# Differential attention in 32 fixed steps of TensorE, with norms of seven heads together and RoPE on POOL

## The chip, the cores and the metric

The kernel runs on one core of one Trainium2 chip. A core has a matrix engine (TensorE, PE in the profile, with its weight loads as PEld), a vector engine (VectorE, DVE), an activation engine (ScalarE, ACT), a general engine (GpSimd, POOL) and SyncE (SP), which here issues all transfers. Each engine takes its own queue of instructions in order and meets the others through semaphores. TensorE reads SBUF and accumulates into the banks of PSUM; VectorE and ScalarE read both. The metric is the time on the device in microseconds, the median of several runs; lower is better.

## The reference, cut to what matters

Two layers of an encoder trunk over 512 tokens of width 1024. Each layer projects the residual stream once and feeds three branches: an SSD scan, a differential attention and a cross-attention into 256 memory tokens. Gates merge the three, an output projection and a LayerNorm close the layer. The change touches the second branch alone:

```python
q = _apply_rope(dq.reshape(Bsz, S, DIFF_HEADS, 2, DIFF_HEAD_DIM), cos, sin)
k = _apply_rope(dk.reshape(Bsz, S, DIFF_HEADS, 2, DIFF_HEAD_DIM), cos, sin)
v = dv.reshape(Bsz, S, DIFF_HEADS, 2 * DIFF_HEAD_DIM)
o = _diff_attention(q, k, v, lam)     # per head: (softmax(q0 k0) - lam * softmax(q1 k1)) v
o = _rmsnorm(o, diff_norm_w[layer]) * (1.0 - lambda_init)
y_diff = o.reshape(Bsz, S, DIFF_WIDTH) * jax.nn.silu(dg.astype(jnp.float32))
```

There are 8 heads. Each has two 64-wide maps (the 128 rows of a head's Q and K hold both) and a 128-wide value.

## The kernel before

**Numbers in two parts.** Every product keeps float32 accuracy by splitting both operands into a high and a low part (`split`, line 95: ScalarE rounds the high part, VectorE subtracts it) and adding three matmuls (`mm3`, line 107: low x high, high x low, high x high).

**Units of weight.** All large matrices come in units of 128 x 1024 numbers, 512 KB each. A plan lists functions with the unit that each needs (`T`, line 130). `emit` (line 133) walks it, and issues the loads (`wr`, two buffers) and splits (`wh`, `wl`, three buffers) of units two places ahead of their use. A projection (`proj`, line 161) takes one unit: 8 x 3 matmuls of 512 columns into one bank `pj`. V projections (`proj_tok`, line 174) take 48 matmuls of 256 columns per unit.

**Order of the work.** The framework orders the instructions of each engine by priorities, which follow the program's order, and by its own estimate of when operands and buffers are ready. `late(n)` (line 100) lowers a priority by `n` places. Inside `manual_schedule(engines={PE})` TensorE's instructions keep the order of the program among themselves; before the change that is used for the six score matmuls of a chunk (lines 866 to 871) and in the SSD branch. Transfers wait in SyncE's one queue in the order in which they were put there.

**The differential attention** (`diff`, line 779). The letters of `ORDER` (line 47, `"qk01vw"` and `"qkg01G"`) list the jobs of an even and of an odd place h:

- `rope` (line 804) projects Q or K of a head. ScalarE copies it out of PSUM (`rx`, line 810), four transfers swap the halves of each 64 rows (`rsw<-rx`, line 813), three VectorE instructions form x cos + swap(x) sin (lines 815 to 817), and `split` makes the two parts `q` or `k`.
- `vpart`, `gpart`: V of two heads, and the SiLU gate of a head (`sdy`).
- `att(h, qp)` (line 848) does two chunks of 128 queries. For each: six score matmuls, three products for each of two maps, into two of the four banks `pm`; a minimum over keys and an exponential with its sum for each map; the weighted difference (line 879); four transposes through the one bank `pt` (line 882); the split into `wT`. Then 12 matmuls with V (line 888) into a bank `po`, which a head holds from its first half to its second.
- At the end of each head (lines 892 to 912): square, four matmuls with a column of ones for the sum of squares, a chain of small VectorE instructions for the norm factor `r` (a 128 x 4 tile), and a transfer that writes it transposed to DRAM (`rd`). For the last head four matmuls spread `r` over a bank instead.
- `fin(h)` (line 915), among the gates of the branch's output (`branch_out`, line 642): broadcasts a head's `rd` to all partitions (`fth<-rd`), multiplies, and splits into `dy`, the input of the branch's projection.

Of the kernel before, what the change touches and what calls it, by code (L numbers as in the profile page):

```python
# [44 lines left out]
LX, LA, LD, LS = 70, 15, 80, 80  # L45

ORDER = ("qk01vw", "qkg01G")
# [10 lines left out]
class Net:  # L58
# [583 lines left out]
    def branch_out(self, l, pool, i, ub, y, tags, after=None, fin=None):  # L642

        st = {}
# [22 lines left out]
        for j in range(KC):  # L667
            if (i, j) in self.ahead_gates:
                self.T(r(j))
            else:  # L670
                self.T(g(j), (l, UGL + 8 * i + j))
            if fin is not None:
                self.T(fin(j))
# [105 lines left out]
    def diff(self, l):  # L779
# [3 lines left out]
        def begin():  # L783
# [17 lines left out]
            self.qk, self.v, self.rd = {}, {}, {}  # L801
            self.sdy = self.t(fp, [P, KC, S], "sdy", bufs=1)

        def rope(h, nm):
            def f(wh, wl):
                fp = self.fp
                ps = self.proj(wh, wl)
# [6 lines left out]
                o = self.t(fp, [P, S], "ro", bufs=1)  # L814
                self.tt(o, x, self.cos, ALU.mult)
                self.tt(sw, sw, self.sin, ALU.mult)
                self.tt(o, o, sw, ALU.add)

                self.qk[h, nm] = [self.t(fp, [P, S], f"{nm}{i}", F32R) for i in range(2)]
                self.split(*self.qk[h, nm], o)  # L820
            return f

        def vpart(h):
            def f(wh, wl):
                if h % 2 == 0:
                    self.vps = [self.bank(self.pj, "pj") for _ in range(2)]
                self.proj_tok(h % 2, wh, wl, *self.rows(self.xh, self.xl), self.vps)
# [8 lines left out]
            return f  # L836

        def gpart(h):
            def f(wh, wl):
                fp = self.fp  # L840
                ps = self.proj(wh, wl)
                th = self.t(fp, [P, S], "fth")
                self.act(th, ps, AF.Tanh, scale=0.5)
                g = self.sdy[:, h, :]
                self.stt(g, th, 1.0, ps, ALU.add, ALU.mult)
            return f

        def att(h, qp):
            def f():
                fp = self.fp  # L850
                (qh, ql), (kh, kl) = self.qk[h, "q"], self.qk[h, "k"]
                v, y = self.v[h], self.sdy[:, h, :]
                if qp == 0:
                    self.po = self.bank(self.pm, "pm")
                    self.s0 = self.t(fp, [P, 4], "fs0")
                po, s0 = self.po, self.s0
                wT = [self.t(fp, [P, 4, 2 * P], f"wT{i}", F32R) for i in range(2)]
                for i in range(2):
                    qc = 2 * qp + i
                    qs = slice(qc * P, (qc + 1) * P)  # L860
                    mx = self.t(fp, [P, 2], "fmx")
                    sm = self.t(fp, [P, 2], "fsm")
                    pp = self.t(fp, [P, 2, S], "fpp")

                    pss = [self.bank(self.pm, "pm") for _ in range(2)]
                    with self.tc.manual_schedule(engines={mybir.EngineType.PE}):
                        for n, (a, b) in enumerate(((ql, kh), (qh, kl), (qh, kh))):
                            for c in range(2):
                                rows = slice(64 * c, 64 * c + 64)
                                with self.late(-LS if n or c else 0):  # L870
                                    self.mm(pss[c], a[rows, qs], b[rows, :], n == 0, n == 2)
                    for c, ps in enumerate(pss):
                        nc.vector.tensor_reduce(out=mx[:, c:c + 1], in_=ps, axis=AX.X, op=ALU.min)  # L873
                        self.act(pp[:, c, :], ps, AF.Exp, scale=-1.0, bias=mx[:, c:c + 1],
                                 accum_out=s0[:, qc:qc + 1] if c == 0 else sm[:, 1:2])

                    nc.vector.reciprocal(out=sm[:, 1:2], in_=sm[:, 1:2])
                    self.ts(sm[:, 1:2], sm[:, 1:2], s0[:, qc:qc + 1], ALU.mult, self.nlam, ALU.mult)
                    self.stt(pp[:, 0, :], pp[:, 1, :], sm[:, 1:2], pp[:, 0, :], ALU.mult, ALU.add)
                    pt = self.bank(self.pt, "pt")  # L880
                    for kc in range(4):
                        self.tr(pt[:, kc * P:(kc + 1) * P], pp[:, 0, kc * P:(kc + 1) * P])
                    o = slice(i * P, (i + 1) * P)
                    self.split(wT[0][:, :, o], wT[1][:, :, o], pt.rearrange("p (k q) -> p k q", k=4))
                with self.late(LA):
                    for kc in range(4):
                        e = slice(kc * P, (kc + 1) * P)
                        self.mm3(po[:, 2 * qp * P:2 * (qp + 1) * P], v[0][:, e], v[1][:, e],
                                 wT[0][:, kc, :], wT[1][:, kc, :], kc == 0, kc == 3)
                if qp == 0:  # L890
                    return
                sq = self.t(fp, [P, S], "fth")
                self.act(sq, po, AF.Square)
                self.stt(y, po, self.dnw, y, ALU.mult, ALU.mult)
                pt = self.bank(self.pt, "pt")
                for c in range(4):
                    self.mm(pt[:, c:c + 1], sq[:, c * P:(c + 1) * P], self.ones[:, 0:1])
                nc.vector.reciprocal(out=s0, in_=s0)
                ms = self.t(fp, [P, 4], "fms")
                self.stt(ms, pt[:, 0:4], 1.0 / 128.0, s0, ALU.mult, ALU.mult)  # L900
                self.tt(ms, ms, s0, ALU.mult)
                self.ts(ms, ms, EPS, ALU.add)
                r = self.rsqrt(fp, ms, 4)
                self.tt(r, r, s0, ALU.mult)
                if h == KC - 1:

                    self.rd[h] = self.bank(self.pm, "pm")
                    for c in range(4):
                        self.mm(self.rd[h][:, c * P:(c + 1) * P], bc(r[:, c:c + 1], [P, P]), self.ident)
                    return  # L910
                self.rd[h] = self.t(self.dp, [4, P], "rd")
                nc.sync.dma_start(out=self.rd[h].rearrange("c p -> p c"), in_=r)
            return f

        def fin(h):
            def f():
                y = self.sdy[:, h, :]
                rb = self.rd.pop(h)
                if h < KC - 1:
                    rb, src = self.t(self.fp, [P, S], "fth"), rb  # L920
                    nc.sync.dma_start(out=rb, in_=src.rearrange("c p -> (c p)")[None, :].broadcast_to([P, S]))
                self.tt(y, y, rb, ALU.mult)
# [235 lines left out]
```

## Time and profile before

| what | value |
|---|---|
| median of 3 runs | 2261.18 us (2260.1 to 2263.97) |
| the profiled execution's own time | 2259.95 us |
| its span, first to last instruction | 2258.2 us |
| mean granted TensorE clock | 0.991 |
| TensorE busy | 2188.9 us (97%) |
| VectorE busy | 1607.9 us (71%) |
| ScalarE busy | 997.7 us (44%) |
| POOL busy | 54.1 us (2%) |
| moved by DMA | 283.80 MB, 126 GB/s |

The profile's page gives busy time, a coarse picture in 40 slices, the chain of work that ended last (followed back from the last instruction) and the costliest groups of instructions. A group's row names line, engine, operation, out<-in tiles and shapes, then how often, busy time, mean duration in ns, and the engine's idle time just before with what ended it. A line can be that of a helper: line 105 is every matmul, 113 every transpose, 83, 86 and 90 VectorE or POOL helpers, 93 every ScalarE activation, so groups are told apart by their tiles. The ends of matmuls are modelled and overlap; the distance from start to start tells their rate. A view by stretches has the busy time of PE, PEld, DVE, ACT and POOL in that order, then the mean granted TensorE clock, the share of DMA time and GB/s.

### The profile page before, as it was taken

The numbers are of one execution on the slowest core, as the hardware profiler recorded it, in microseconds if no ns is written. First come the engines' busy times: TensorE is split into PE (matmuls) and PEld (weight loads), VectorE is DVE, ScalarE is ACT, GpSimd is POOL, SyncE is SP. The second block draws the span as 40 slices with busy tenths as digits, with TensorE's granted clock in tenths as the row PEclk, the third lists the DMA queues.
The fourth block names the chain that finished last, engine by engine and source line by source line (L and its number), as shares of the span: only waits on it lengthen the run. The fifth ranks groups of instructions, "written<-read, shape, count | busy, mean of one in ns | idle before, by whom it ended". The sixth has DMA issues, their size and how long they took to land.

```text
span 2258.2 us, 30602 instructions
## 1 busy us (share of the span) xinstructions
PE 2188.9 (97%) x11712; PEld 1798.9 (80%) x11712; DVE 1607.9 (71%) x2672; ACT 997.7 (44%) x1877; POOL 54.1 (2%) x38
## 2 busy tenths in 40 slices
PE   8999999999999999999999999999999999989998
PEld 6787877788888777878997778787788887778788
DVE  7987888758545767766568878888744547677667
ACT  5664555424432444443355565454423324444430
POOL 0000000100000000000000101010100000000000
PEclk9999999999999999999999999999999999999999
DMA  4654444435453333434564645353443332343343
GB/s 147 182 163 149 136 142 133 131 97 178 154 173 112 79 84 75 75 79 137 162 223 111 178 128 155 123 163 113 127 140 108 107 113 71 85 71 80 78 137 126
DMA packets 115587, 283.80 MB, mean 126 GB/s; under 512 B 19952, under 2 KB 24560, under 8 KB 115184
## 3 DMA queue, kind: packets, MB, share of 16 engines
q1 hardware_dynamic: 115440, 281.84, 43.3%
q8 instruction: 92, 1.51, 0.3%
q14 instruction: 55, 0.45, 0.1%
HBM read 255.55 MB, written 17.85 MB: 121 GB/s over the span
## 4 chain that ended last, share of the span: by engine, by line
PE 73%; DVE 14%; DMA 7%; ACT 3%; issue 2%; SPq 1%; POOL 0%; POOLq 0%; DVEq 0%; ACTq 0%
PE pj L105 60%; PE pm L105 9%; PE pt L113 3%; DMA ab<-dab 3%; DVE wl L83 2%; DVE fmx L873 2%; DMA rsw<-rx 2%; DVE ab L83 2%; DVE acc L86 1%; DMA wr<-wu 1%; DVE y L83 1%; ACT ab L93 1%; SPq L813 1%; PE pt L105 1%; DVE yl L86 1%
## 5 line engine op out<-in xcount | busy, mean ns | idle before, releaser
L105 PE MATMUL pj<-xh,wl 128*128 128x512 f32 x1664 | 665.4, 400 | 10.5 <-DVE wl L83 8.5
L105 PE MATMUL pj<-xh,wh 128*128 128x512 f32 x1664 | 665.6, 400 | 0.0
L105 PE MATMUL pj<-xl,wh 128*128 128x512 f32 x1664 | 662.6, 398 | 0.0
L83 DVE TENSOR_TENSOR wl<-wr,wh 128x1024 fp32r<-128x1024 f32 x330 | 404.3, 1226 | 93.4 <-ACT wh L93 93.1
L93 ACT ACTIVATE wh<-wr 128x1024 fp32r<-128x1024 f32 x330 | 347.6, 1054 | 238.9 <-PE pj L105 191.9
L105 PEld LDWEIGHTS pj<-xh,wl 128*128 128x128 f32 x1664 | 316.4, 190 | 81.8 <-issue 7.0
L105 PEld LDWEIGHTS pj<-xh,wh 128*128 128x128 f32 x1664 | 315.8, 190 | 68.6 <-issue 6.4
L105 PEld LDWEIGHTS pj<-xl,wh 128*128 128x128 f32 x1664 | 315.9, 190 | 65.2 <-issue 4.1
L93 ACT ACTIVATE ab<-ab,bias 128x128 f32<-128x128 f32 x512 | 160.8, 392 | 114.8 <-DVE ab L83 114.0
L86 DVE SCALAR_TENSOR_TENSOR acc<-pj,hcw,acc 128x510 f32<-128x510 f32 x192 | 142.3, 743 | 24.0 <-ACT acc L93 22.9
L93 ACT ACTIVATE fpp<-pm,fmx 128x512 f32<-128x512 f32 x128 | 87.2, 685 | 72.6 <-DVE fmx L873 70.8
L105 PE MATMUL pj<-yl,wh 128*128 128x512 f32 x256 | 102.6, 401 | 0.8 <-DVE yl L86 0.8
L105 PE MATMUL pj<-yh,wh 128*128 128x512 f32 x256 | 103.1, 403 | 0.0
L105 PE MATMUL pj<-yh,wl 128*128 128x512 f32 x256 | 102.1, 400 | 0.0
L105 PE MATMUL pj<-dy,wh 128*128 128x512 f32 (+1 forms) x384 | 102.0, 354 | 0.0
L83 DVE TENSOR_TENSOR ab<-ab,cst 128x1024 f32<-128x1024 f32 x64 | 86.4, 1351 | 18.1 <-DMA ab<-dab 17.8
L873 DVE TENSOR_REDUCE fmx<-pm 128x1 f32<-128x512 f32 x128 | 85.2, 683 | 11.3 <-PE pm L105 11.3
L105 PE MATMUL pj<-cy,wh 128*128 128x512 f32 x256 | 78.8, 389 | 0.0
L105 PEld LDWEIGHTS pj<-dy,wh 128*128 128x128 f32 x384 | 67.9, 189 | 10.0
L105 PE MATMUL pj<-wh,xh 128*128 128x256 f32 x256 | 73.4, 287 | 0.0
L83 POOL TENSOR_TENSOR sqa<-sqa,sz 128x512 f32<-128x512 f32 x32 | 52.8, 1650 | 843.8 <-ACT sz L93 843.8
L105 PE MATMUL pj<-wh,xl 128*128 128x256 f32 x256 | 73.0, 285 | 0.0
(269 smaller groups left out, 3457.8 us busy)
## 6 DMA issues: line engine op xcount, KB each, us to landing
wr<-wu SPq DMA_DIRECT2D x336, 512.0 KB, 3.6
ab<-dab SPq DMA_DIRECT2D x64, 512.0 KB, 5.7
eb<-deb SPq DMA_DIRECT2D x64, 256.0 KB, 4.7
mkv<-dkv SPq DMA_DIRECT2D x16, 512.0 KB, 4.2
rsw<-rx SPq DMA_DIRECT2D x128, 64.0 KB, 2.0
dgt<-tg SPq DMA_DIRECT2D x18, 256.0 KB, 2.5
dkv<-mo SPq DMA_DIRECT2D x16, 256.0 KB, 4.1
dkv<-q SPq DMA_DIRECT2D x16, 256.0 KB, 3.7
```

What stands on the lines that cost most here:

```text
L83: (eng or self.nc.vector).tensor_tensor(out=out, in0=a, in1=b, op=op)
L86: self.nc.vector.scalar_tensor_tensor(out=out, in0=a, scalar=s, in1=b, op0=op0, op1=op1)
L93: self.nc.scalar.activation(out=out, in_=a, func=f, **kw)
L105: self.nc.tensor.matmul(out=out, lhsT=a, rhs=b, start=first, stop=last)
L113: self.nc.tensor.transpose(out=out, in_=x, identity=self.ident)
L813: nc.sync.dma_start(out=sw[32 * i:32 * i + 32], in_=x[32 * (i ^ 1):32 * (i ^ 1) + 32])
L873: nc.vector.tensor_reduce(out=mx[:, c:c + 1], in_=ps, axis=AX.X, op=ALU.min)
```

## The change

The differential attention's instructions on TensorE get one fixed order, from the first Q projection to the last gate of this branch, under one `manual_schedule`. The projections of this stretch are cut in halves of 12 matmuls (`proj2` and `vpart` are generators). 35 steps take one unit each: 28 projections of Q, K, V and SiLU gates of the next heads, then the seven branch gates that `branch_out` made before. The first 32 steps go with the 32 chunks of the attention (8 heads of 4 chunks). Step s issues the scores of chunk s + 1, half a projection, the values part of an earlier pair of chunks where one is due, the transposes of chunk s, and the other half. A head's sums of squares follow the scores of a later step.

The norm factors of heads 0 to 6 are formed at once in step 30, as a tile of 28 columns, transposed by TensorE through `pt`, and written to DRAM in rows; the last head keeps its own. `fin` comes for two heads a step in steps 31 to 34. RoPE's two products and its sum go from VectorE to POOL, in place, without the tile `ro`.

```diff
-LX, LA, LD, LS = 70, 15, 80, 80
-
-ORDER = ("qk01vw", "qkg01G")
+LX, LD = 70, 80
...
+    def proj2(self, wh, wl):
+
+        ps = self.bank(self.pj, "pj")
+        for k in range(KC):
+            if k == KC // 2:
+                yield
+            c = slice(k * P, (k + 1) * P)
+            self.mm3(ps, wh[:, c], wl[:, c], self.xh[:, k, :], self.xl[:, k, :], k == 0, k == KC - 1)
+        return ps
...
+            self.s0, self.ss = (self.t(fp, [P, 4 * KC], f"fs{i}", bufs=1) for i in range(2))
...
-                ps = self.proj(wh, wl)
+                ps = yield from self.proj2(wh, wl)
...
-                o = self.t(fp, [P, S], "ro", bufs=1)
-                self.tt(o, x, self.cos, ALU.mult)
-                self.tt(sw, sw, self.sin, ALU.mult)
-                self.tt(o, o, sw, ALU.add)
+                self.tt(x, x, self.cos, ALU.mult, nc.gpsimd)
+                self.tt(sw, sw, self.sin, ALU.mult, nc.gpsimd)
+                self.tt(x, x, sw, ALU.add, nc.gpsimd)
...
-                self.split(*self.qk[h, nm], o)
-            return f
+                self.split(*self.qk[h, nm], x)
+            return f, (l, (UQ if nm == "q" else UK) + h)
...
-                self.proj_tok(h % 2, wh, wl, *self.rows(self.xh, self.xl), self.vps)
+                x = self.rows(self.xh, self.xl)
+                self.proj_tok(h % 2, wh, wl, *x, self.vps[:1], (0, 1))
+                yield
+                self.proj_tok(h % 2, wh, wl, *x, self.vps[1:], (2, 3))
...
+        def gate(j):
+            def f(wh, wl):
+                ps = yield from self.proj2(wh, wl)
+                st[j] = self.t(self.fp, [P, S], tags[j // 2], bufs=2)
+                self.act(st[j], ps, AF.Tanh, scale=0.5, bias=self.hgb[:, 8 + j:9 + j])
+            return f, (l, UGL + 8 + j)
...
+        def scores(s):
+            h, qc = divmod(s, 4)
...
+            pss = [self.bank(self.pm, "pm") for _ in range(2)]
+            for n, (a, b) in enumerate(((ql, kh), (qh, kl), (qh, kh))):
+                for c in range(2):
+                    rows = slice(64 * c, 64 * c + 64)
+                    self.mm(pss[c], a[rows, qs], b[rows, :], n == 0, n == 2)
...
+        def turn(s):
...
+            pp, pt = self.pp.pop(s), self.bank(self.pt, "pt")
+            for kc in range(4):
+                self.tr(pt[:, kc * P:(kc + 1) * P], pp[:, 0, kc * P:(kc + 1) * P])
+            o = slice(i * P, (i + 1) * P)
+            self.split(self.wT[0][:, :, o], self.wT[1][:, :, o], pt.rearrange("p (k q) -> p k q", k=4))
...
+        def sums(h):
+            pt = self.bank(self.pt, "pt")
+            for c in range(4):
+                self.mm(pt[:, c:c + 1], self.sq[:, c * P:(c + 1) * P], self.ones[:, 0:1])
+            self.act(self.ss[:, 4 * h:4 * h + 4], pt[:, 0:4])
...
+        def norms():
+
+            n = 4 * (KC - 1)
+            r = norm(0, KC - 1)
+            pt = self.bank(self.pt, "pt")
+            self.tr(pt[:n, :P], r)
+            rt = self.t(self.fp, [n, P], "rt", bufs=1)
+            self.act(rt, pt[:n, :P])
+            self.rd = self.t(self.dp, [n, P], "rd")
+            nc.sync.dma_start(out=self.rd, in_=rt)
...
+        def step(unit, *parts):
+
+            def f(wh, wl):
+                g = fn(wh, wl)
+                for p in parts:
+                    for job in p:
+                        job()
+                    next(g, None)
+            fn, u = unit
+            self.T(f, u)
...
+        self.T(lambda: order.enter_context(self.tc.manual_schedule(engines={mybir.EngineType.PE})))
+        step(rope(0, "q"), (), ())
+        step(rope(0, "k"), (), ())
+        step(vpart(0), (), ())
+        step(vpart(1), (), (job(scores, 0),))
+        units = []
+        for h in range(KC):
+            if h + 1 < KC:
+                units += [rope(h + 1, "q"), rope(h + 1, "k")]
+                units += [gpart(h), gpart(h + 1)] if h % 2 == 0 else [vpart(h + 1), vpart(h + 2)]
+        gates = [j for j in range(KC) if (1, j) not in self.ahead_gates]
+        units += [gate(j) for j in gates]
+        nst = 4 * KC
+        for s, unit in enumerate(units):
+            first = [job(scores, s + 1)] if s + 1 < nst else []
+            amid = []
+            if s % 4 == 2 and s < nst:
+                amid.append(job(values, s // 4, 0))
+            if s % 4 == 0 and 0 < s <= nst:
+                amid.append(job(values, s // 4 - 1, 1))
+            if s < nst:
+                amid.append(job(turn, s))
+            if s % 4 == 1 and 1 < s <= nst + 1:
+                first.append(job(sums, s // 4 - 1))
+            if s == nst - 2:
+                amid.append(norms)
+            if s == nst + 1:
+                amid.append(last)
+            step(unit, first, amid)
+            if s >= nst - 1:
+                for h in range(2 * (s - nst + 1), min(2 * (s - nst + 1) + 2, KC)):
+                    self.T(job(fin, h))
+        self.T(order.close)
```

More of the change, by code (lines that the diff above doesn't have):

```diff
@@ L640, in gate_ahead, with branch_out @@
         self.T(f, (l, UGL + 8 * i + j))
-    def branch_out(self, l, pool, i, ub, y, tags, after=None, fin=None):
-        st = {}
+    def branch_out(self, l, pool, i, ub, y, tags, after=None, st=None):
+        done, st = st is not None, {} if st is None else st
         def g(j):
@@ L846, in gpart @@
[L846 to L893, printed above, removed]
-                self.stt(y, po, self.dnw, y, ALU.mult, ALU.mult)
[L895 to L913, printed above, removed]
@@ new lines, in norms, with last @@
+        def norms():
[7 more added lines that the diff above has]
+            nc.sync.dma_start(out=self.rd, in_=rt)
+        def last():
+            r = norm(KC - 1, KC)
+            self.rb = self.bank(self.pm, "pm")
+            for c in range(4):
+                self.mm(self.rb[:, c * P:(c + 1) * P], bc(r[:, c:c + 1], [P, P]), self.ident)
```

94 lines of the change are left out of this document (61 added, 33 removed).

## The prediction

> **What bounds the kernel now.** I read the page first: shares of the engines, then the chain of work that ended last.
>
> ```profile
> span 2258.2 us, 30602 instructions
> PE 2188.9 (97%) x11712; PEld 1798.9 (80%) x11712; DVE 1607.9 (71%) x2672; ACT 997.7 (44%) x1877; POOL 54.1 (2%) x38
> PE 73%; DVE 14%; DMA 7%; ACT 3%; issue 2%; SPq 1%; POOL 0%; POOLq 0%; DVEq 0%; ACTq 0%
> PE pj L105 60%; PE pm L105 9%; PE pt L113 3%; DMA ab<-dab 3%; DVE wl L83 2%; DVE fmx L873 2%; DMA rsw<-rx 2%; DVE ab L83 2%; DVE acc L86 1%; DMA wr<-wu 1%; DVE y L83 1%; ACT ab L93 1%; SPq L813 1%; PE pt L105 1%; DVE yl L86 1%
> ```
>
> TensorE bounds the kernel, so a gain must be TensorE time that is lost now. The two differential attentions lie at 711 to 1033 us and 1833 to 2166 us (from RoPE's first projection to the last gate, about). The busy time by stretch, and TensorE's waits inside each, show what is lost there:
>
> ```profile
> 711.00:1033.00 322.00, 307.33 (x1717) 248.78 (x1716) 225.84 (x486) 143.96 (x278) 0.00 (x0) 0.98 0.38 86
> 1833.00:2166.00 333.00, 316.17 (x1751) 255.80 (x1750) 227.97 (x489) 146.76 (x281) 0.00 (x0) 0.98 0.37 86
> ```
>
> ```profile
> PE pt L113 <- DVE fsm L877: 11.3, 3, 4.4
> PE pt L113 <- DVE rs_y L86: 1.7, 3, 0.6
> ...
> PE pt L113 <- DVE fsm L877: 13.9, 3, 5.3
> PE pt L113 <- DVE rs_y L86: 1.7, 3, 0.6
> ```
>
> The columns of the waits are total, times, longest. In each layer the transposes of the softmax weights (line 113) wait three times for a long while and three times briefly: 11.3 + 1.7 + 13.9 + 1.7 = 28.6 us. The long ones cost twice, because the granted clock drops right behind them. Of six windows around the six long waits, the first and the last:
>
> ```profile
> 824.50:831.40 6.90, 3.68 (x12) 2.94 (x13) 5.20 (x11) 3.22 (x8) 0.00 (x0) 0.75 0.26 76
> ...
> 2094.60:2101.20 6.60, 3.02 (x10) 2.55 (x10) 6.37 (x12) 3.51 (x8) 0.00 (x0) 0.74 0.25 79
> ```
>
> 6.9 x 0.25 = 1.7 us of clock is lost behind each, 10 us for six; the clock column 0.98 of the two whole stretches says 0.02 x 655 = 13 us, rounded. I take 12. So 28.6 + 12 = 40.6 us can be won.
>
> Why the long ones? Followed around 895 us (the SyncE queue, VectorE and the chain of waits in this window, and the two transfers in the list of DMA issues, whose last column is us to landing):
>
> ```profile
> 882.51 0.38 SPq L912 DMA_DIRECT2D rd<-rs_y  x1
> 884.00 2.41 SPq L813 DMA_DIRECT2D rsw<-rx  x4
> ...
> 892.70 0.69 DVE L83 TENSOR_TENSOR rsw<-rsw,sin 128x512 f32<-128x512 f32 x1 [5.19 <-DMA rsw<-rx]
> ...
> 885.82 6.75 DMA rsw<-rx
> ...
> 899.77 1.08 PE pt L113 x4
> ...
> rsw<-rx SPq DMA_DIRECT2D x128, 64.0 KB, 2.0
> ...
> rd<-rs_y SPq DMA_DIRECT2D x14, 2.0 KB, 9.8
> ```
>
> A head's norm factors go out as one transfer of 2 KB (`rd`, a transposing write of single numbers) that takes 9.8 us. The half swaps of the next K stand behind it in the same queue and land 6.75 us after their issue, not 2.0. VectorE meanwhile stands at RoPE's sine product, and the score reductions behind it in its queue wait too; the transposes of those scores are the 4.4 us wait.
>
> **The change part by part.**
>
> (1) Seven norms together. Of eight norm chains a layer two are left, one 28 columns wide, and the seven slow `rd` transfers go; one transfer of 28 rows of 512 B takes their place. With this the cause of the six long waits goes: 11.3 + 13.9 + 12 = 37.2 us.
>
> (2) TensorE's order by hand: scores of the next chunk, half a projection, the transposes of this chunk, the other half. A chunk's transposes now stand a whole step and half a projection behind its scores. What a step is, from matmul starts in two timelines (27 matmuls of 512 columns lie between the first two rows, 36 of 256 columns between the last two of the four behind):
>
> ```profile
> 882.27 0.39 PE L105 MATMUL pj<-xh,wh 128*128 128x512 f32 x1
> ...
> 888.39 0.39 PE L105 MATMUL pj<-xh,wh 128*128 128x512 f32 x1
> ...
> 849.55 1.66 PE L105 MATMUL pm<-k,q 64*128 64x512 f32 x12
> 851.14 0.39 PE L105 MATMUL pj<-wh,xl 128*128 128x256 f32 x1
> 851.36 0.28 PE L105 MATMUL pj<-wl,xh 128*128 128x256 f32 x1
> ...
> 855.67 0.28 PE L105 MATMUL pj<-wl,xh 128*128 128x256 f32 x1
> ...
> 785.61 0.63 PE L113 MATMUL pt<-cst,fpp 128*128 128x128 f32 x4 [0.55 <-DVE rs_y L86]
> ```
>
> So 0.227 us a matmul of 512 columns, 0.12 of 256, 1.59 us twelve score matmuls, 0.63 us four transposes. A step is 24 x 0.227 + 0.8 + 0.63 = 6.9 us, with a values part (12 x 0.12) 8.3. The transposes come about 10 us behind their scores; the softmax between (two reductions, two exponentials, one product) has room, so the six short waits, 3.4 us, go as well. The number of matmuls stays, but the scores, now and then twelve in a row, are always six between projections: 851.14 to 851.36 is 0.1 us more than its kind, and I allow as much for the way in. Some five more such passages a layer: +1 us in both.
>
> (3) RoPE's three instructions go to POOL. VectorE loses 48 of this group's kind a layer:
>
> ```profile
> L83 DVE TENSOR_TENSOR rsw<-rsw,sin 128x512 f32<-128x512 f32 x32 | 22.1, 691 | 41.4 <-DMA rsw<-rx 41.3
> ...
> L83 POOL TENSOR_TENSOR sqa<-sqa,sz x32: 1286/1534/2659, 91.5 to 1621.9; 128x512 f32<-128x512 f32 x32
> ...
> 223.26 1.29 POOL L83 TENSOR_TENSOR sqa<-sqa,sz 128x512 f32<-128x512 f32 x1 [12.12 <-ACT sz L93]
> 223.30 2.34 DVE L83 TENSOR_TENSOR ab<-ab,cst 128x1024 f32<-128x1024 f32 x1
> ...
> L83 DVE TENSOR_TENSOR ab<-ab,cst x64: 1207/1220/2343, 65.9 to 1608.1; 128x1024 f32<-128x1024 f32 x64
> ...
> 416.39 2.11 POOL L83 TENSOR_TENSOR sqa<-sqa,sz 128x512 f32<-128x512 f32 x1 [70.32 <-ACT sz L93]
> ```
>
> The same shape on POOL takes 1.29 us undisturbed, and it and VectorE's instructions with both inputs in SBUF hold each other up: the VectorE one took 2.34 us behind it, where its group's median is 1.22; the other way round POOL took 2.11, 0.82 more. POOL has nothing else in these stretches (its 0.00 in the rows above); six such instructions a head, 8 to 13 us of some 30, wait in its queue only for each other. VectorE's load: 33 us a layer less, at most 48 x 1.29 = 62 us more in blocking: 226 - 33 + 62 = 255 us in some 300, still not the bound. And its queue no longer stands at the swap's landing.
>
> What is late next is K. The order by hand gives the K projection of the next head one step, that with a values part, before its scores stand at TensorE's head; every later matmul is queued behind them. From the start of the copy out of PSUM (which is when the step begins), with these rows:
>
> ```profile
> 718.01 0.60 ACT L93 ACTIVATE rx<-pj 128x512 f32<-128x512 f32 x1 [2.07 <-PE pj L105]
> ...
> 722.61 0.69 DVE L83 TENSOR_TENSOR rsw<-rsw,sin 128x512 f32<-128x512 f32 x1 [1.79 <-DMA rsw<-rx]
> ...
> L83 DVE TENSOR_TENSOR k<-ro,k 128x512 fp32r<-128x512 f32 x16 | 11.0, 686 | 0.1
> ...
> L93 ACT ACTIVATE k<-ro 128x512 fp32r<-128x512 f32 x16 | 10.0, 624 | 18.3 <-DVE ro L83 18.3
> ```
>
> the sine product can begin at 4.6 us (the cosine product lies before it, beside the swaps), then 1.29 + 1.29 on POOL, 0.62 on ScalarE, 0.69 on VectorE, and 0.3 I add for four handovers: 8.8 us. TensorE asks for K's low part at 8.3 + 0.2 + one score pair 0.23 = 8.7 us (0.3 later where the step holds a V projection, 48 x 0.12). So bare, the wait is 0 to 0.1 us. Upper bound: both POOL instructions blocked once (2 x 0.82) and the subtraction behind POOL (2.34 - 1.22) gives 2.8. I take 0.7, about one block a head, as VectorE has two or three such instructions a step: 16 heads x 0.7 = +11 us. Below nothing it can't go.
>
> ScalarE gets a copy of each head's sums besides; it is busy 144 of 322 us in the first stretch, which covers that.
>
> (4) The joint norm transposes through the one `pt` bank right behind a chunk's own transposes, so it waits for that bank to be read, two conversions like K's (0.62 + 0.69, with handovers 1.5): +3 us in both layers. Zero if the norm were put elsewhere; at most some 3 us each, if its small VectorE chain is late as well. The last head's own norm, the gates and the broadcasts of `rd` keep their kind; the broadcasts now come two a step over four steps, behind gates on TensorE for 20 us and more, and are costed at nothing.
>
> Sum, against the profiled execution's own 2259.95 us: - 37.2 - 3.4 + 1 + 11 + 3 = -25.6, so 2234.4; the median of the runs, 2261.18, stands 1.2 us above that execution: **2236 us**.
>
> **The rivals.**
>
> *K late at every head (slower).* If POOL and VectorE block each other at each of the chain's instructions, the wait is the 2.8 us bound at each of 16 heads, and the clock may drop behind it. For that speaks a place elsewhere in this trace, the wait and the window around it:
>
> ```profile
> 1295.56 0.69 PE L105 MATMUL pm<-m,xsT 128*64 128x128 f32 x4 [1.97 <-DVE m L83]
> ...
> 1293.50:1299.10 5.60, 3.63 (x23) 3.13 (x23) 4.70 (x9) 1.11 (x2) 0.00 (x0) 0.70 0.64 173
> ```
>
> 16 x (2.8 + 1.7) = 72 instead of 11: 2297 us. It decides from (40.6 - 4) / 16 = 2.3 us a head on, clock included. Against it: the chain's last pieces meet VectorE's reductions and subtractions out of PSUM, which do not block. The Trainium skill, "TensorE: Matmul & The Clock Gate", section "Why this matters for your kernels", lets the clock fall only at idle gaps over about 3 us; by that rule the 2.8 us waits would cost no clock and this rival 16 x 2.8 = 45, so 2270 us. The trace disagrees: 1.97 us idle was followed by the half clock.
>
> *The swaps stay late.* If `rd` is not what holds them up but the weights in the same queue, the six long waits come back, on POOL instead of VectorE: +37, 2273 us. Against it: where no `rd` lies ahead, as at 718 us, the sine product starts 4.6 us behind the copy.
>
> *No new wait.* K is in time everywhere and the norm's wait hidden: 14 us better, 2222 us.
>
> **How the numbers follow.** My forecast (2224 to 2252 us) has 0.66, no new wait 0.12, late K 0.13, late swaps 0.04, and 0.05 goes to gain and loss cancelling. A measurement can tell 0.2% (4.5 us) from no change. Faster: 0.66 + 0.12 = 0.78; same 0.05; slower 0.17. The range 2214 to 2262 reaches some 8 us below the case without waits, for what the order by hand may win besides, and leaves the two slower cases out; my forecast's own is the narrower one given with its chance.
>
> **What would show it.** Right: no `rd` transfers between the swaps, swaps landing some 2 us after issue, no wait of transposes for `fsm`, six clock drops fewer, POOL near 54 + 96 x 1.3 to 2.1 = 180 to 255 us, and TensorE waiting, if at all, at the first scores of a head for K, below 1.5 us. Wrong: waits of scores for K over 2.3 us, or a wait for VectorE at the transposes of most steps.

## The result, and the profile after

The changed kernel takes 2318.1 us (median; 2311.2 to 2320.0) against 2261.4 us before: 1.0244 times, 95% interval 1.0221 to 1.0267. It is slower. The forecast was 2236 us, range 2214 to 2262: wrong in sign as well as in size. The profiled execution of the changed kernel took 2320.0 us.

From the page of the changed kernel, the span with the engines' shares and the chain that ended last by engine and by line (helper lines moved by the edit: a matmul is line 103 now, a transpose 111, VectorE and POOL products 81, 84 and 88, ScalarE 91):

```profile
span 2318.2 us, 30418 instructions
PE 2207.5 (95%) x11714; PEld 1814.8 (78%) x11714; DVE 1557.4 (67%) x2372; ACT 1003.4 (43%) x1895; POOL 189.1 (8%) x134
PE 68%; DVE 11%; DMA 8%; POOL 6%; ACT 4%; issue 2%; SPq 2%; POOLq 0%; DVEq 0%; ACTq 0%
```

POOL, 0% of the chain before, now holds 6% of it with 189 us of work: the new place of RoPE lies on the path that sets the end. What TensorE waits for (total, times, longest), in the changed kernel:

```profile
PE pm L103 <- ACT k L91: 50.6, 16, 4.6
PE pm L103 <- DVE rs_y L81: 16.5, 2, 8.5
...
PE pt L111 <- DVE wT L81: 2.8, 2, 1.4
...
PE pm L103 <- DVE k L81: 2.5, 11, 0.2
```

Three readings. The waits of transposes for `fsm` and `rs_y`, 28.6 us before, are gone without rest. In their place the scores of every head wait for K: 50.6 us for the high part and 2.5 for the low, 3.3 us a head. And twice TensorE stands 8 us at the last head's own norm (`rs_y`), which the forecast counted at nothing.

The differential attention as one stretch, from the load of `lam` to the first matmul of the branch's own projection, by layer: first before, then after. After the two times come its length, the busy time of PE, PEld, DVE, ACT and POOL, the granted clock, the share of DMA and GB/s.

```profile
710.10:1033.50 323.40, 308.73 (x1724) 249.94 (x1723) 225.84 (x486) 143.96 (x278) 0.00 (x0) 0.98 0.38 86
1832.70:2159.60 326.90, 310.07 (x1724) 250.73 (x1723) 226.03 (x486) 144.43 (x278) 0.00 (x0) 0.98 0.37 85
```

```profile
707.70:1063.10 355.40, 320.81 (x1725) 260.67 (x1725) 203.93 (x336) 147.03 (x287) 69.22 (x48) 0.93 0.26 79
1863.00:2220.40 357.40, 319.52 (x1724) 260.07 (x1723) 197.44 (x336) 147.12 (x287) 67.24 (x48) 0.94 0.26 78
```

The stretch is 32.0 + 30.5 = 62.5 us longer in both layers, the span 60.0: all of the loss is here. The clock fell from 0.98 to 0.93 and 0.94, because it drops behind the new waits as it did behind the old ones. VectorE has 22 to 29 us less work a layer, as meant, and that bought nothing.

**One head, followed.** The changed kernel's timeline, 893 to 917 us, POOL, then ScalarE, VectorE, a piece of the chain of waits in this stretch (the last swap of Q), and TensorE. A row has start, duration, engine and line, operation, and in brackets the idle time before it with what ended it.

```profile
900.41 1.28 POOL L81 TENSOR_TENSOR rx<-rx,cos 128x512 f32<-128x512 f32 x1 [24.13 <-DMA rsw<-rx]
901.66 1.75 POOL L81 TENSOR_TENSOR rsw<-rsw,sin 128x512 f32<-128x512 f32 x1
903.49 1.28 POOL L81 TENSOR_TENSOR rx<-rx,rsw 128x512 f32<-128x512 f32 x1
910.10 1.30 POOL L81 TENSOR_TENSOR rx<-rx,cos 128x512 f32<-128x512 f32 x1 [5.33 <-DVE fsm L88]
911.36 1.72 POOL L81 TENSOR_TENSOR rsw<-rsw,sin 128x512 f32<-128x512 f32 x1
913.15 1.26 POOL L81 TENSOR_TENSOR rx<-rx,rsw 128x512 f32<-128x512 f32 x1
```

```profile
895.71 0.60 ACT L91 ACTIVATE rx<-pj 128x512 f32<-128x512 f32 x1 [2.13 <-PE pj L103]
...
904.81 0.63 ACT L91 ACTIVATE q<-rx 128x512 fp32r<-128x512 f32 x1 [3.29 <-POOL rx L81]
905.34 0.58 ACT L91 ACTIVATE rx<-pj 128x512 f32<-128x512 f32 x1
...
914.44 0.63 ACT L91 ACTIVATE k<-rx 128x512 fp32r<-128x512 f32 x1 [4.41 <-POOL rx L81]
```

```profile
910.08 1.86 DVE L84 SCALAR_TENSOR_TENSOR fpp<-fpp,fsm 128x512 f32<-128x512 f32 x1
```

```profile
898.20 2.05 DMA rsw<-rx
```

```profile
895.28 0.39 PE L103 MATMUL pj<-xh,wh 128*128 128x512 f32 x1
...
903.26 0.39 PE L103 MATMUL pj<-xh,wh 128*128 128x512 f32 x1
...
915.13 0.50 PE L103 MATMUL pm<-k,q 64*128 64x512 f32 x2 [3.00 <-ACT k L91]
915.85 0.73 PE L103 MATMUL pm<-k,q 64*128 64x512 f32 x4 [0.23 <-DVE k L81]
```

The first POOL triple is Q's, the second K's. Both cosine products start 4.7 to 4.8 us behind the copy out of PSUM (895.71 to 900.41, 905.34 to 910.10), and Q's 0.16 us after the last of the four swaps has landed (898.20 + 2.05 = 900.25). The forecast had them start beside the swaps. They can't: the product is written in place, over the tile `rx` that the swaps are still reading. (For K's product the profile names `fsm`, a VectorE instruction on other tiles that ended in the same moment.) Then ScalarE, which takes its instructions in order, stands 3.29 us at Q's late sum, and the copy of K out of PSUM is queued behind it: it starts at 905.34, 2.08 us behind the start of K's last matmul (903.26), where Q's copy had started 0.43 us behind Q's (895.28 to 895.71). So K's copy is some 1.65 us late before K's own chain begins. (The expectation of experiment 1 takes 1.9.)

**The last norm.** The same kernel, 1034 to 1060 us: SyncE's queue, ScalarE's copy of the sums of squares, VectorE's queue, TensorE.

```profile
1035.23 5.22 SPq L954 DMA_DIRECT2D fth<-rd  x3
```

```profile
1040.87 0.16 ACT L91 ACTIVATE fs<-pt 128x4 f32<-128x4 f32 x1
```

```profile
1042.76 0.69 DVE L81 TENSOR_TENSOR sdy<-sdy,fth 128x512 f32<-128x512 f32 x1 [0.44 <-DMA fth<-rd]
1043.36 0.15 DVE L84 SCALAR_TENSOR_TENSOR fs<-fs,fs 128x4 f32<-128x4 f32 x1
...
1047.90 0.69 DVE L81 TENSOR_TENSOR sdy<-sdy,fth 128x512 f32<-128x512 f32 x1 [1.07 <-DMA fth<-rd]
...
1050.77 0.16 DVE L81 TENSOR_TENSOR rs_y<-rs_y,fs 128x4 f32<-128x4 f32 x1
```

```profile
1050.98 2.08 PE L103 MATMUL pm<-cst,rs_y 128*128 128x128 f32 x8 [8.54 <-DVE rs_y L81]
```

The sums are there at 1041.0, and the chain of small VectorE instructions, 0.16 us each, ends at 1050.9. Among them in VectorE's queue stand the products of the broadcasts of the other heads, 0.69 us each, and two of those wait for their own transfers. TensorE, in its fixed order, has nothing it may do meanwhile.

**The ledger** against the forecast's sum, in us over both layers. The clock lost is half of each time spent at clock 0.50 while TensorE did not wait.

| term | forecast | measured |
|---|---|---|
| old waits at the transposes, with the clock behind them | -40.6 | about -39 (28.5 waits, 10.5 clock) |
| passages between projections and scores | +1 | about -8 |
| K late, with its clock | +11 | +87 (53.1 waits, some 34 clock) |
| joint norm at the bank `pt` | +3 | +2.8 |
| last head's norm, with its clock | 0 | about +22 |
| smaller waits, and outside the stretch | 0 | about -5 |

### The profile page after: what moved, and what is told of

It is laid out like the page before. It is cut to its first block, busy times and chain, and to the rows that moved or that the text cites. A ratio compares the mean times of both kernels' runs of the same rounds, so it can differ in the third digit from the quotient of the medians.

```text
span 2318.2 us, 30418 instructions
## 1 busy us (share of the span) xinstructions
PE 2207.5 (95%) x11714; PEld 1814.8 (78%) x11714; DVE 1557.4 (67%) x2372; ACT 1003.4 (43%) x1895; POOL 189.1 (8%) x134
## 4 chain that ended last, share of the span: by engine, by line
PE 68%; DVE 11%; DMA 8%; POOL 6%; ACT 4%; issue 2%; SPq 2%; POOLq 0%; DVEq 0%; ACTq 0%
PE pj L103 57%; PE pm L103 9%; DMA ab<-dab 4%; POOL rx L81 3%; DVE wl L81 2%; POOL rsw L81 2%; PE pt L111 2%; DVE ab L81 2%; DMA rsw<-rx 2%; SPq L820 1%; DVE acc L84 1%; ACT wh L91 1%; ACT rx L91 1%; DVE y L81 1%; DMA wr<-wu 1%
## 5 line engine op out<-in xcount | busy, mean ns | idle before, releaser
L103 PE MATMUL pj<-xh,wl 128*128 128x512 f32 x1664 | 677.0, 407 | 9.7 <-DVE wl L81 7.9
L103 PE MATMUL pm<-k,q 64*128 64x512 f32 x384 | 69.8, 458 | 53.1 <-ACT k L91 50.6
L81 POOL TENSOR_TENSOR rx<-rx,cos 128x512 f32<-128x512 f32 x32 | 43.5, 1359 | 894.4 <-DMA rsw<-rx 725.7
L103 PEld LDWEIGHTS pm<-k,q 64*128 64x128 f32 x384 | 32.6, 193 | 81.1 <-ACT k L91 55.7
L103 PE MATMUL pj<-wh,xl 128*128 128x256 f32 x256 | 81.2, 317 | 0.0
```

The lines of the kernel that those rows point to most:

```text
L81: (eng or self.nc.vector).tensor_tensor(out=out, in0=a, in1=b, op=op)
L103: self.nc.tensor.matmul(out=out, lhsT=a, rhs=b, start=first, stop=last)
```

## The experiments

Theory A: K is late because RoPE's cosine product writes over the tile that the swaps read, so that it waits for them, once in Q's chain and once in K's. The rival B: POOL is too slow, and too much held up by VectorE, for a chain with one step of time, in place or not. Both leave the last norm to a cause of its own. Each ratio is against the kernel before, timed on the same chip.

### 1. The cosine product in a tile of its own

```diff
-                self.tt(x, x, self.cos, ALU.mult, nc.gpsimd)
+                o = self.t(fp, [P, S], "ro", bufs=1)
+                self.tt(o, x, self.cos, ALU.mult, nc.gpsimd)
                 self.tt(sw, sw, self.sin, ALU.mult, nc.gpsimd)
-                self.tt(x, x, sw, ALU.add, nc.gpsimd)
+                self.tt(o, o, sw, ALU.add, nc.gpsimd)
```

> One part of the change undone: the cosine product goes to a tile of its own instead of over its input; RoPE stays on POOL. Theory A (in place): the four swap transfers read the input, so the product that overwrites it starts only when they have landed (it started 4.7 us behind the copy in the changed kernel, not 0.6), and the late Q part holds up the copy of K in ScalarE's queue by 1.9 us. Then the wait of scores for K falls from 3.3 us a head to under 1 us, 53 us of waits to under 16, most of some 35 us of half clock goes: 2318 - 37 - 28, about 2250 us. Theory B (port): POOL and VectorE hold each other up, and the place of the cosine product matters little: over 2 us a head stay, about 2300 us.

Measured 2248.4 us, ratio 0.9932 (0.9915 to 0.9950): from 2.4% slower to 0.7% faster by one tile of 128 x 512. Its waits of TensorE, and POOL's timeline for one head:

```profile
PE pm L103 <- DVE rs_y L81: 16.3, 2, 8.3
...
PE pm L103 <- ACT k L91: 8.1, 8, 1.9
...
PE pm L103 <- DVE k L81: 3.7, 16, 0.3
```

```profile
876.47 1.27 POOL L81 TENSOR_TENSOR ro<-rx,cos 128x512 f32<-128x512 f32 x1 [17.77 <-ACT rx L91]
880.50 1.29 POOL L81 TENSOR_TENSOR rsw<-rsw,sin 128x512 f32<-128x512 f32 x1 [2.76 <-DMA rsw<-rx]
```

The cosine product starts 0.68 us behind the copy (875.79) and is done long before the swaps land. K's waits fall from 53.1 to 11.8 us, as theory A has it for RoPE on POOL. The last norm's 16 us are untouched, so that is another cause.

### 2. RoPE back on VectorE, with the tile

```diff
-                self.tt(o, x, self.cos, ALU.mult, nc.gpsimd)
-                self.tt(sw, sw, self.sin, ALU.mult, nc.gpsimd)
-                self.tt(o, o, sw, ALU.add, nc.gpsimd)
+                self.tt(o, x, self.cos, ALU.mult)
+                self.tt(sw, sw, self.sin, ALU.mult)
+                self.tt(o, o, sw, ALU.add)
```

(against experiment 1)

> One part of the change undone: RoPE's three instructions back on VectorE, with a tile of their own; fixed order and joint norms stay. Theory A and theory B both: the chain is as in the kernel before, K's parts ready some 7 to 8.5 us behind the copy, no wait of scores for K over 0.5 us, 53 + 35 us gone: about 2232 us, the wait of the last head's norm (16.5 us and its clock) left. Theory C (the order by hand leaves too little room for any RoPE): waits for K of 2 us a head stay, about 2290 us.

Measured 2232.8 us, ratio 0.9864 (0.9837 to 0.9891). No wait of scores for K is left; the one for the last norm is the largest of all:

```profile
PE pm L103 <- DVE rs_y L81: 16.5, 2, 8.4
```

So fixed order and joint norm, without RoPE on POOL, gain 1.4% with the last norm's loss still in it. On POOL with its own tile RoPE costs 16 us more than on VectorE: B has this much.

### 3. In place, but on VectorE

```diff
-                self.tt(x, x, self.cos, ALU.mult, nc.gpsimd)
-                self.tt(sw, sw, self.sin, ALU.mult, nc.gpsimd)
-                self.tt(x, x, sw, ALU.add, nc.gpsimd)
+                self.tt(x, x, self.cos, ALU.mult)
+                self.tt(sw, sw, self.sin, ALU.mult)
+                self.tt(x, x, sw, ALU.add)
```

(against the changed kernel)

> The changed kernel with RoPE in place but on VectorE. Theory A: the cosine product waits for the swaps here as well, but it is 0.7 us and not 1.3 and nothing of POOL lies in the chain: K's low part some 8 to 8.5 us behind the copy, waits for K under 1 us a head, 2235 to 2250 us. If the in-place product were enough by itself, whatever the engine: over 2280 us.

Measured 2240.6 us, ratio 0.9932 (0.9917 to 0.9947). TensorE's waits for K:

```profile
PE pm L103 <- DVE k L81: 2.2, 10, 0.2
```

In place alone costs 8 us over experiment 2, or 0.7 points of ratio (the two ran on different chips). The waits for K are 2.2 us of it; where the rest lies was not followed. POOL alone (experiment 1) costs 16 us, both together 85. From K's copy to the end of its low part the chain takes 7.8 us in experiment 2 (877.50 to 885.26), 8.95 in experiment 1, 9.2 here (880.99 to 890.17) and 10.5 in the changed kernel (905.34 to 915.80). So the two costs add up in one chain, and only past the step's end do they turn into waits.

There is a second difference. With RoPE on VectorE, K's copy stands ahead of Q's high part in ScalarE's queue (they start at 880.99 and 882.43 here); with RoPE on POOL it stands behind, so Q's lateness reaches K only there. Neither A nor B alone is the cause.

### 4. Room of one step

Q and K of the following heads are projected one step earlier (Q of head 1 already ahead of its V); RoPE stays in place on POOL.

```diff
         step(vpart(0), (), ())
+        step(rope(1, "q"), (), ())
         step(vpart(1), (), (job(scores, 0),))
...
             if h + 1 < KC:
-                units += [rope(h + 1, "q"), rope(h + 1, "k")]
+                units.append(rope(h + 1, "k"))
                 units += [gpart(h), gpart(h + 1)] if h % 2 == 0 else [vpart(h + 1), vpart(h + 2)]
+            if h + 2 < KC:
+                units.append(rope(h + 2, "q"))
...
-                for h in range(2 * (s - nst + 1), min(2 * (s - nst + 1) + 2, KC)):
+                for h in range(2 * (s - nst + 1), min(2 * (s - nst + 1) + 2, KC) if s < nst + 1 else KC):
```

> The changed kernel, RoPE in place on POOL as it is, only that the Q and K projections of the next head come one step earlier in the fixed order (Q of head 1 already before V of head 1), so K has two steps before its scores and not one. Theory A: the chain is 10 us long from copy to low part, two steps are 15: no wait of scores for K, 53 us of waits and some 35 us of half clock gone, about 2230 us. Theory B (port): POOL's 60 us a layer hold up VectorE, waits of transposes or scores for the softmax appear in their place, over 2270 us.

Measured 2211.3 us, ratio 0.9802 (0.9785 to 0.9820), below A's 2230 us, which left the last norm's wait in. The group of scores among the costliest groups (busy, mean ns, idle before them), and the first layer's stretch:

```profile
L103 PE MATMUL pm<-k,q 64*128 64x512 f32 x384 | 61.7, 426 | 0.0
```

```profile
707.10:1004.20 297.10, 295.69 (x1704) 242.95 (x1703) 188.54 (x310) 141.73 (x282) 68.33 (x48) 1.00 0.29 91
```

RoPE's chain is as long as in the changed kernel (ScalarE stands at POOL's sum for K 67.5 us, at Q's 45.5), and nothing on TensorE waits for it: clock 1.00. The wait at the last norm is gone too. The fixed order is a step shorter and ends with that norm's step, and 33 matmuls of the branch's projection, which lie outside the fixed order, stand ahead of it in TensorE's queue:

```profile
L103 PE MATMUL pj<-dy,wh 128*128 128x512 f32 x21 | 6.5, 392 | 0.0
```

(the larger of their groups, between 1004 and 1013 us; 12 more take `wl`). Its span, 2204.7 us, is 113.5 us shorter than the changed kernel's; K's 87 and the last norm's 22 are 109 of it. (The two ran on different chips; by their ratios to the kernel before the difference is 0.044, some 100 us.)

### 5. The same room, RoPE on VectorE

Experiment 4 with the edits of experiments 1 and 2.

> Q and K projections one step earlier, and RoPE on VectorE with a tile of its own: what POOL is worth where the order leaves room. Theory A: with two steps of room K is in time on either engine, so within 0.5% of the one with RoPE on POOL (2211 us). If POOL's relief of VectorE counted, this one would be slower by more than that.

Measured 2209.4 us, ratio 0.9797 (0.9780 to 0.9813), not distinguishable from experiment 4. Where the order leaves room, RoPE in place on POOL and RoPE on VectorE with its own tile cost the same; VectorE's relief is worth nothing that these intervals can show.

### 6. The same room, joint norm earlier

```diff
             if s == nst - 2:
-                amid.append(norms)
+                first.append(norms)
```

(against experiment 4; the joint norm's transpose then stands ahead of its step's four)

> Q and K one step earlier, RoPE in place on POOL, and the joint norm at the start of step 30 instead of behind its transposes. It no longer waits for the one bank of the transposes: 1.4 us a layer less, 2208 us, and the broadcasts of the joint norm start some 4 us earlier. If VectorE's chain of small instructions is not done by then, TensorE waits for it instead, up to 3 us a layer.

Measured 2210.4 us, ratio 0.9792 (0.9774 to 0.9810). The 2.8 us wait at `pt` is gone and each stretch is 295.5 us long, 1.6 less than in experiment 4; in the total that can't be told from nothing.

### 7. The slow transfer alone

The kernel before; each head's norm factors are transposed by TensorE and written in rows of 512 bytes. Nothing else is changed.

```diff
+                pt = self.bank(self.pt, "pt")
+                self.tr(pt[:4, :P], r)
+                rt = self.t(fp, [4, P], "rt")
+                self.act(rt, pt[:4, :P])
                 self.rd[h] = self.t(self.dp, [4, P], "rd")
-                nc.sync.dma_start(out=self.rd[h].rearrange("c p -> p c"), in_=r)
+                nc.sync.dma_start(out=self.rd[h], in_=rt)
```

> The prediction's first step alone: the kernel before, only that each head's norm factors are transposed by TensorE and written to DRAM in rows of 512 bytes instead of single numbers. Theory: this transfer held up the swaps behind it; it lands in about 2 us, the six long waits of transposes (25.2 us) and 12 us of half clock go, less some 2 us for eight more transposes and copies a layer: about 2226 us. Rival (the weights in the same queue hold the swaps up): 2261 us.

Measured 2236.2 us, ratio 0.9875 (0.9845 to 0.9905), 27 us won, where 35 were expected: some short waits stay, and the wait for the last norm grows from 0.7 to 4.1 us. The wait of transposes for `fsm`, 25.2 us in six before:

```profile
PE pt L113 <- DVE fsm L877: 5.9, 10, 0.8
```

The longest is now 0.8 us, not 5.3. This was the cause the forecast named for the six long waits, and the four lines that remove it are worth as much as the forecast gave the whole change.

### 8. RoPE on POOL alone, in place

The kernel before, with the changed kernel's three POOL lines.

> One part of the change alone: the kernel before with RoPE on POOL, in place as in the change. Theory A: TensorE's order by priorities puts other work between K and its scores, so the longer chain costs little, and VectorE no longer stands at the swaps (41.3 us of its waits): the long waits shrink, but the slow transfer of the norm factors stays in front of the swaps and makes K late at three heads a layer: 2245 to 2275 us. Theory B: every head loses: over 2280 us.

Measured 2362.6 us, ratio 1.0437 (1.0408 to 1.0466), far above what A expected; B's figure came. What TensorE waits for here, then ScalarE:

```profile
PE pm L105 <- ACT wT L93: 40.0, 6, 8.2
PE pt L113 <- DVE fsm L876: 38.7, 6, 7.3
PE pt L113 <- DVE fpp L86: 21.5, 8, 3.2
```

```profile
ACT k L93 <- POOL rx L83: 83.1, 16, 10.0
ACT q L93 <- POOL rx L83: 72.4, 16, 7.0
```

ScalarE stands at POOL 155 us in all, and the exponentials and the conversions of `wT` stand in the same queue. The median swap now takes longer to land; its row in the list of DMA issues (last column), 2.0 before:

```profile
rsw<-rx SPq DMA_DIRECT2D x128, 64.0 KB, 5.2
```

### 9. RoPE on POOL alone, with its own tile

Experiment 8 with `ro` as in experiment 1.

> The kernel before with RoPE on POOL, and the cosine product in a tile of its own. Theory A (in place): most of the 100 us that RoPE on POOL in place cost the kernel before goes; the slow transfer of the norm factors still makes three K a layer late, by some 2 us more than on VectorE: 2260 to 2285 us. Theory B (POOL's slower instructions and the port): over 2320 us.

Measured 2339.4 us, ratio 1.0373 (1.0352 to 1.0393): A's expectation failed again, and B's figure came. The largest of TensorE's waits, 40.0 us in experiment 8, is hardly smaller:

```profile
PE pm L105 <- ACT wT L93: 33.4, 6, 7.6
```

In the old order the tile saves only 0.6 points of ratio, some 14 us (23 by the medians, which come from two chips). Here the seven slow `rd` writes are still there, and at many heads the swaps land 8 to 14 us behind the copy instead of 4.5. ScalarE and VectorE then stand one after the other at the late RoPE (VectorE 64.7 us at K's high part). How much of the 3.7% is the late swaps, and how much the queues behind a POOL that is slower in any case, no run separates; it stays open. Taken alone, the move to POOL is a loss in the old order, in place or not.

### 10. Broadcasts earlier

The changed kernel; the broadcasts `fth<-rd` go into the four buffers of Q, which are free by then, heads 0 to 3 in step 31 and 4 to 6 in step 32.

```diff
-                rb = self.t(self.fp, [P, S], "fth")
+                rb = self.t(self.fp, [P, S], ("q0", "q1")[h % 2])
...
-            if s >= nst - 1:
-                for h in range(2 * (s - nst + 1), min(2 * (s - nst + 1) + 2, KC)):
-                    self.T(job(fin, h))
+            for h in {nst - 1: (0, 1, 2, 3), nst: (4, 5, 6), nst + 2: (7,)}.get(s, ()):
+                self.T(job(fin, h))
```

> The changed kernel, only that the broadcasts of the joint norm go into four buffers that are free by then (those of Q) instead of two that the square and the gate share, and come for four heads after step 31 and three after step 32 instead of two a step. Theory D (queue): the last head's small norm chain stands in VectorE's queue among products that wait for late broadcasts; with these early, TensorE's wait for the last norm falls from 8 us a layer to 1 or 2, and 10 us of half clock with it: 2318 - 13 - 9, about 2296 us. Rival: the chain is late by itself (sums, copy, seventeen small instructions), then 2318 us.

Measured 2307.3 us, ratio 1.0233 (1.0215 to 1.0251).

```profile
PE pm L103 <- DVE rs_y L81: 7.4, 2, 3.9
```

The wait at the last norm is more than halved, from 16.5 to 7.4 us, so the broadcasts in VectorE's queue are a cause of it. The chain of small instructions, unbroken here, takes 2.9 us (1038.85 to 1041.77) instead of 7.6 (1043.36 to 1050.93). What stays is the rival's part: the sums are there at 1037.7, and one split of a weight and the chain itself come before TensorE can go on. By the ratio almost nothing shows: the intervals of this kernel and of the changed one overlap.

### 11. and 12. All mends in the short order

Experiment 10 with the joint norm as the first thing in step 31 and the last norm in step 34, and with RoPE as in experiment 1 (on POOL) or as in experiment 2 (on VectorE).

```diff
-            if s == nst - 2:
-                amid.append(norms)
-            if s == nst + 1:
-                amid.append(last)
+            if s == nst - 1:
+                first.append(norms)
+            if s == nst + 2:
+                first.append(last)
```

> Three repairs of the changed kernel together, RoPE on POOL: cosine product in a tile of its own, early broadcasts in four buffers, and the joint norm moved behind the scores of step 31's place (so it does not wait for the bank of the transposes) with the last head's norm one step later. From the run with the own tile, 2248 us: less 16 us of waits for the last norm, some 8 us of half clock, 2.8 us of waits for the bank: about 2222 us; 12 us of waits for K stay.

> The same three repairs with RoPE's instructions on VectorE instead of POOL. From the run with RoPE back on VectorE, 2233 us: less 16.5 and 2.8 us of waits and some 8 us of half clock: about 2207 us. If POOL were worth its place (VectorE relieved), this one would be slower than the one on POOL.

Measured 2239.4 us, ratio 0.9928 (0.9910 to 0.9947), on POOL, and 2221.2 us, 0.9847 (0.9827 to 0.9867), on VectorE: both miss by 14 to 17 us, and by their ratios neither can be told from experiments 1 and 2, on which they build. The last norm still waits, 9.6 us in the first and 10.0 in the second; of the second:

```profile
PE pm L103 <- DVE rs_y L81: 10.0, 2, 5.2
```

I had expected these to vanish. Since the joint norm comes a step later, so do the broadcasts. Their products and splits now stand ahead of the last norm's chain in VectorE's queue: in the second kernel the sums are there at 1000.9 and the chain begins at 1004.94. What one move gives, the other takes back. Experiment 4 has the chain about as broken as the changed kernel, but lets other matmuls stand ahead of it, and there the wait is gone.

## Why the prediction was wrong

**Step 1, seven norms together: right.** The waits named have gone, and experiment 7 shows that the slow `rd` write was their cause.

**Step 2, the order by hand: right on the softmax, wrong on the passages.** All waits of the transposes went. I added 1 us for passages between matmuls of different kinds; in fact TensorE's own work in the stretch became shorter. Without idle time and lost clock the first layer's took 303.9 us before (323.4, less 14.7 idle and 4.8 of clock) and 300.0 after (355.4, less 34.6 and 20.8; clock lost during a wait isn't counted twice). The group of value matmuls, before and then after (busy time, mean ns), shows the place:

```profile
L105 PE MATMUL pm<-wT,v 128*128 128x256 f32 x192 | 32.1, 295 | 0.1
```

```profile
L103 PE MATMUL pm<-wT,v 128*128 128x256 f32 x192 | 25.6, 282 | 0.0
```

Before, some were issued singly between others; now they always come twelve in a row. Other passages give back 2 to 3 us a layer of these 6.5.

**Step 3, RoPE on POOL: this is where it failed.** The sentence is "the cosine product lies before it, beside the swaps". The diff says "in place"; I used it for the tile `ro` that goes, and did not ask who else still reads `rx`. A write waits for all readers, and four of those were transfers. That puts 1.3 us into K's chain and 1.3 into Q's. Q's part I did not follow at all: it reaches K through ScalarE's queue, where K's copy stands behind Q's high part. With the tile of its own, K's copy comes 8.3 us behind Q's (875.79 to 884.06 in experiment 1), in the changed kernel 9.6 (895.71 to 905.34). The bare chain was sized well: with the tile, K's low part is ready 8.95 us behind its copy, where I had 8.8. The waits for K are then 8.1 + 3.7 = 11.8 us, where I had 11, but that the totals agree is luck: I had 0.7 us at each head, and measured are 0.2 to 0.5 at ten heads and 1.0 to 2.2 at six.

That VectorE and POOL hold each other up was foreseen and is seen: the `fpp` product that began together with POOL's cosine product (910.08 and 910.10) took 1.86 us, 0.75 alone, and POOL's sine product right behind took 1.72 instead of 1.29. The Trainium skill, "SBUF — State Buffer", section "Who interferes with whom", gives the cause as a pair of ports that the two share under an exclusive lock; the rows agree.

**Step 4, the joint norm: right** (2.8 us for 3). **The last norm, "costed at nothing": wrong**, 16.5 us and some 6 of clock. I named a cover (the gates on TensorE) for the broadcasts, but not for the norm. Moving it into a fixed order took from TensorE what it could do meanwhile, and moving the broadcasts put their products, and their waits for transfers, among its small instructions in VectorE's queue (experiments 4 and 10).

**The rival "K late at every head"** is what came, with a chance of 0.13, but by another mechanism than the one it named. Its bound of 2.8 us a head was passed, 3.3, since it was built from POOL's blocking alone; its price with the clock was 4.5 a head and is 87 / 16 = 5.4. The point from which it was to decide, 2.3 us a head, held. "Late swaps" did not come, and "no new wait" came only in the experiments that gave the chain a step of room.

## What to carry to other kernels

Before an operation is made in place, list every reader of the tile, transfers too: the write started only when the last was done, and in a chain with one step of time that cost 70 us here with the products on POOL, 8 with them on VectorE. A chain that crosses engines reaches its neighbour through each in-order queue that it passes, so follow Q's lateness into K's copy and the broadcasts into the norm. A fixed order of the bounding engine should issue what feeds a step with a whole step to spare (2211 us instead of 2318 with the same work), and leave independent work outside it, before any thought is given to which engine does the small products.

## What the runs showed of the hardware

The clock drops behind waits much shorter than I would have minded. One of 1.94 us and one of 2.76 us in the changed kernel (TensorE's timeline), and the stretches behind them:

```profile
731.64 0.50 PE L103 MATMUL pm<-k,q 64*128 64x512 f32 x2 [1.94 <-ACT k L91]
...
877.00 0.80 PE L103 MATMUL pm<-k,q 64*128 64x512 f32 x2 [2.76 <-ACT k L91]
```

```profile
732.90:736.30 3.40, 3.40 (x17) 3.22 (x16) 2.46 (x6) 1.61 (x5) 0.00 (x0) 0.50 0.01 2
...
876.20:883.10 6.90, 6.10 (x26) 5.01 (x26) 3.56 (x6) 3.02 (x6) 0.09 (x1) 0.51 0.24 78
```

Half clock for 3.4 us in the one case and 6.8 in the other: 1.7 or up to 3.4 us lost behind a wait of 2 to 3. Behind all 16 waits for K, 1.9 to 4.6 us long, the clock fell so; behind the two of 1.4 us at the joint norm it did not. All 18 spells of half clock in the two stretches of the changed kernel last one, two or three times 3.41 us, and their starts lie whole multiples of 3.41 us apart (732.90 and 763.62 are nine apart), wherever the waits end. So what a wait costs depends also on where it falls in this grid: another wait of 2.76 us, at 2034.93, was followed by 3.4 us of half clock only.

The Trainium skill, "TensorE: Matmul & The Clock Gate", section "Why this matters for your kernels", sets the limit at gaps of about 3 us. That fits eight of the waits for K; the other eight were shorter than 3.0 us, and the one of 1.94 us, like that of 1.97 us in the prediction, speaks against it.
